# Sums of the output projection's last column block kept in PSUM between passes, and the first normalised chunks split in two halves from an fp32 copy

## The chip, the cores and the metric

The kernel runs on one core of one Trainium2 chip. The metric is the device time in microseconds of one execution, the median of several runs.

## What is computed

A two-layer encoder over 256 positions with a width of 2048, all in fp32. One layer, cut to what matters here:

```
h   = rmsnorm(x, pre_mix_norm)
proj = h @ w_in
o_a = mla_mixer(...)            # attention, 1024 channels
o_b = conformer_conv(...)       # convolution + layernorm + silu, 512 channels
o_c = gdn_mixer(...)            # gated delta rule, 512 channels
mix = concat(o_a, o_b, o_c) @ w_out
x   = x + rmsnorm(mix, post_mix_norm)
h   = rmsnorm(x, pre_ffn_norm)
f   = (silu(h @ w_gate) * (h @ w_up)) @ w_down
x   = x + rmsnorm(f, post_ffn_norm)
```

## The kernel before

Everything lies in one program. The 256 rows are two tiles of 128 (`t` = 0 and 1). Every fp32 matrix product is made of three passes on TensorE: both operands are split into a high and a low half, `hi` (a cast on ScalarE, the ACT engine, `hilo` L328) and `lo` (a subtraction on VectorE, the DVE engine, L329), and a chunk of 128 input channels takes the matmuls L353 (hi by hi), L354 (lo by hi) and L355 (hi by lo).

- `dense()` (L337) is the product of 256 rows with a block of 512 columns. A unit is two chunks: one DMA brings the weights (`ws`), ACT makes `wh` (L328, 128x1024), DVE makes `wl` (L329, 128x1024), then 12 matmuls follow. The sums lie in two PSUM tiles of the pool `psa` (four banks, tag `acc`); at the end `evac` takes them out.
- The other four PSUM banks are the pool `psb` (tag `tp`, function `TP()` L76). All transposes and all the side work of the mixer (heads, convolution, delta rule) go through these four.
- `norm_quad(t, g, ...)` (L435) transposes four 128x128 pieces of `xs` into a `tp` bank (L439), multiplies by the gain and splits the outcome. For all quads but the first this is one DVE multiply of 128x512 (L448), one cast and one subtraction (L328, L329 on 128x512). The first quad (t = 0, g = 0) goes in four columns through `hilo_col`: per column ACT L332 (scale and cast, 128x128) and DVE L333 (scale and subtract, 128x128). This happens four times: at the start, at the beginning of the FFN of both layers, and at the beginning of layer 1.
- `out_proj` (L1186 on) multiplies the joined mixer outputs by `w_out`. It goes in two passes over the 16 input chunks, four column blocks (`nb` 0 to 3) in each: pass 0 takes chunks 0 to 7 (attention), pass 1 takes 12 to 15 (delta rule) and 8 to 11 (conformer). After pass 0 the sums are copied out to SBUF (ACT L1197, one per `t`); after pass 1 DVE adds (L1200), ACT squares for the norm (L1203), DVE multiplies by the norm's weight (L1206), and after block 3 `residual` (L490) takes the reciprocal root (L262 to L270) and updates `xs` (L496, four per `t`). The product with `w_down` has one pass only.
- `conformer()` (L922) runs as background work while `out_proj` is in its first pass: 31 multiply-adds on DVE (L949), then for each `t` four transposes into a `tp` bank (L956), mean and variance (L959, L961), the root (L241 to L249) and the normalisation (L964), which reads that `tp` bank again; then eight transposes (L973), SiLU (ACT L978, with a table load), cast and subtraction. Its results are chunks 8 to 11 of `out_proj`.
- `gdn()` ends with four transposes for each `t` (L913) that fill two `tp` banks, split by ACT L332 and DVE L333 in 128x512.
- `token_sums` (L1246) takes the first quad's fp32 values by adding hi and lo again (L1251), once in a layer.

The order of the instructions on each engine is fixed when the program is built, by a scheduler with modelled costs and the pools' free buffers. An engine does its instructions strictly in that order. A weight cast can be told to be issued behind a given instruction (`hold`): at the kernel's start that is the third of the four column casts (`FH = 2`).

Of the kernel before, what the change touches and what calls it, by code (L numbers as in the profile page):

```python
# [13 lines left out]
ALU = mybir.AluOpType  # L14
# [30 lines left out]
QORDER = (4, 0, 5, 1, 6, 2, 7, 3)  # L45
EARLY = 2
UB = 64
FH = 2
SETUP_REST = 2
TURN = 1.5  # L50

# [2 lines left out]
def kernel(  # L54
# [18 lines left out]
    def U(dt=F32):  # L73
        return upool.tile([P, 512], dt, tag="u", name="u")
# [55 lines left out]
    def vcol(l, i, c):  # L130
        if l == 0 and i == PRE_MIX:
            return col0[:, c:c + 1]
        o = voff[(l, i)] + c
        return cols[:, 0, o:o + 1]
# [200 lines left out]
        return ins  # L335

    def dense(lhs, ks, n, load, evac, ch=2, need=None, pre=None, head=0, mid=None, tail=0,  # L337
              after0=None):

        acc = [psa.tile([P, 512], F32, tag="acc", name="acc") for _ in range(NT)]
        nu = -(-len(ks) // ch)
        held = []

        def mm(t, c, u, kc, wh, wl):
            i = u * ch + c
            rh = wh[:, c * n:(c + 1) * n]
            rl = wl[:, c * n:(c + 1) * n]  # L350
            xh, xl = lhs(kc[c], t)
            o = acc[t][:, 0:n]
            pe.matmul(o, xh, rh, start=(i == 0), stop=False)  # L353
            pe.matmul(o, xl, rh, start=False, stop=False)  # L354
            pe.matmul(o, xh, rl, start=False, stop=(i == len(ks) - 1))  # L355

        def unit(u):
            kc = ks[u * ch:(u + 1) * ch]
            m = len(kc)
            ws = wpool.tile([P, 1024], F32, tag="ws", name="ws", bufs=WSB)  # L360
            wv = ws[:, 0:m * n].rearrange("p (c n) -> p c n", c=m)
            load(wv, kc[0], m)
            wh = wpool.tile([P, 1024], F32R, tag="wh", name="wh", bufs=WHB)
            wl = wpool.tile([P, 1024], F32R, tag="wl", name="wl", bufs=WHB)
            with ExitStack() as order:
                if u < head:
                    for u0, ins in hold:
                        if u >= u0:
                            order.enter_context(tc.issue_after(ins.ins))
                hilo(wh[:, 0:m * n], wl[:, 0:m * n], ws[:, 0:m * n])  # L370
            if need is not None:
                for k in kc:
                    bg.ensure(*need(k))
            return u, kc, wh, wl

        for u in range(nu):
            a = unit(u)
            if head <= u < nu - tail:
                for c in range(len(a[1])):
                    for t in range(NT):  # L380
                        mm(t, c, *a)
            else:
                for c in range(len(a[1])):
                    mm(0, c, *a)
                held.append(a)
                if u == head - 1 and mid is not None:
                    mid()
                if u == nu - 1:
                    if pre is not None:
                        pre()  # L390
                        pre = None
                    evac(0, acc[0][:, 0:n])
                if u in (head - 1, nu - 1):
                    for h in held:
                        for c in range(len(h[1])):
                            mm(1, c, *h)
                    held.clear()
            bg.step(BUDGET)
        if pre is not None:
            pre()  # L400
        if after0 is not None:
            after0()
        for t in range(1 if tail else 0, NT):
            evac(t, acc[t][:, 0:n])

# [29 lines left out]
    def norm_quad(t, g, tiles, gain, keep=None):  # L435

        ps = TP()
        for c in range(4):
            pe.transpose(ps[:, c * P:(c + 1) * P], xs[:, t, (4 * g + c) * P:(4 * g + c + 1) * P], ident)  # L439
        hi, lo = U(F32R), U(F32R)  # L440
        if g == 0 and t == 0:
            for c in range(4):
                s = slice(c * P, (c + 1) * P)
                ins = hilo_col(hi[:, s], lo[:, s], ps[:, s], vcol(*gain, c))
                first_hi.append(ins)
        else:
            f = U()
            dve.tensor_tensor(out=v3(f, 4), in0=v3(ps, 4), in1=bc(gain_cols(*gain, 4 * g, 4), 2, P), op=ALU.mult)  # L448
            hilo(hi, lo, f)
            if keep is not None:  # L450
                keep[(g, t)] = f
        tiles[(g, t)] = (hi, lo)

    def ask(tiles, gain, load=None, keep=None):
# [54 lines left out]
    for l in range(DEPTH):  # L509
# [11 lines left out]

        if l == 0:
            norm_quad(0, 0, hT, (0, PRE_MIX))
            hold.append((1, first_hi[FH]))
        K16 = list(range(16))
        rxb = []

# [657 lines left out]
        def out_proj(lhs, passes, w, wpm, rname, need, after0):  # L1185
            parts = {}  # L1186
            ssqp = [SM(4, "ssqp0"), SM(4, "ssqp1")]
            for i, ks in enumerate(passes):
                last = i == len(passes) - 1
                for nb in range(4):  # L1190
                    if i == 0:
                        parts[(nb, 0)], parts[(nb, 1)] = U(), U()

                    def ev(t, ps):
                        o = parts[(nb, t)]
                        if not last:
                            act.copy(out=o, in_=ps)  # L1197
                            return
                        if i > 0:
                            dve.tensor_tensor(out=o, in0=o, in1=ps, op=ALU.add)  # L1200
                            ps = o
                        junk = U()
                        act.activation(out=junk, in_=ps, func=AF.Square, accum_out=ssqp[t][:, nb:nb + 1])  # L1203

                        def weigh():
                            dve.tensor_tensor(out=o, in0=ps, in1=wpm[nb], op=ALU.mult)  # L1206
                        if nb == 3:
                            residual(t, parts, ssqp, rname, weigh)
                        else:
                            weigh()  # L1210
                    dense(lhs, ks[nb], 512, wload(w, nb * 512, 512), ev, need=need,
                          **(dict(tail=TAILG, after0=after0) if last and nb == 3 else {}))


        a, b = list(range(8)), [12, 13, 14, 15, 8, 9, 10, 11]
        passes = [[a[:6], a, a, a], [a[6:] + b, b, b, b]]
        h2, F = {}, {}
        out_proj(lmix, passes, w_out[l], wpm, "rm", need_mix, lambda: norm_quad(0, 0, h2, (l, PRE_FFN)))


        more2 = ask(h2, (l, PRE_FFN), keep=F)
# [19 lines left out]
        def token_sums():  # L1241
# [3 lines left out]

            for g in range(4):  # L1246
                fast = [q for q in range(2) if 2 * g + q in FAST]
                if (g, 0) not in F:
                    F[(g, 0)] = U()
                    hi, lo = h2[(g, 0)]  # L1250
                    dve.tensor_tensor(out=F[(g, 0)], in0=hi.bitcast(F32), in1=lo.bitcast(F32), op=ALU.add)  # L1251
                f0, f1 = [F.pop((g, t)).rearrange("p (q j n) -> p q j n", q=2, j=2) for t in range(NT)]
                d = U()
                dve.tensor_tensor(out=d.rearrange("p (q j n) -> p q j n", q=2, j=2), in0=f0, in1=f1,
# [211 lines left out]
```

## Time and profile before

| what | value |
|---|---|
| time, median of 3 runs | 2232.72 us (2232.12 to 2234.08) |
| time of the profiled execution | 2234.14 us |
| its span in the trace | 2232.4 us |
| granted TensorE clock, mean | 0.996 |
| TensorE busy | 2202.9 us (99%) |
| VectorE busy | 1762.1 us (79%) |
| ScalarE busy | 1183.3 us (53%) |
| DMA, bytes over the span | 407.75 MB, mean 183 GB/s |

The kernel is one long stream of matmuls with few gaps. The span is the profiled execution from its first to its last instruction; its own time lies 1.7 us above it, and 1.4 us above the median of the runs. The line numbers are those of the kernel before. In the rows, PE is TensorE, DVE VectorE, ACT ScalarE; the number in brackets is idle time of that engine just before the instruction, and what ended it. Matmul records that follow each other in a stream overlap, so their distance is read from their starts.

### The profile page before, as it was taken

The numbers are of one execution on the slowest core, as the hardware profiler recorded it, in microseconds if no ns is written. First come the engines' busy times: TensorE is split into PE (matmuls) and PEld (weight loads), VectorE is DVE, ScalarE is ACT, GpSimd is POOL, SyncE is SP. The second block draws the span as 40 slices with busy tenths as digits, with TensorE's granted clock in tenths as the row PEclk, the third lists the DMA queues.
The fourth block names the chain that finished last, engine by engine and source line by source line (L and its number), as shares of the span: only waits on it lengthen the run. The fifth ranks groups of instructions, "written<-read, shape, count | busy, mean of one in ns | idle before, by whom it ended". The sixth has DMA issues, their size and how long they took to land.

```text
span 2232.4 us, 29210 instructions
## 1 busy us (share of the span) xinstructions
PE 2202.9 (99%) x10483; PEld 1841.3 (82%) x10483; DVE 1762.1 (79%) x2873; ACT 1183.3 (53%) x1642; POOL 45.6 (2%) x93
## 2 busy tenths in 40 slices
PE   8999999999999999999999999999999999999998
PEld 7988887788888888888879888877888888888886
DVE  6777998899989897544486879979989998975444
ACT  6665545555555555444356655455555555554442
POOL 2000000000000000000000000000000000000000
PEclk9999999999999999999999999999999999999999
DMA  7554624546656656555556545245566566665553
GB/s 254 172 178 146 188 95 155 163 164 209 216 180 220 223 190 221 173 194 192 179 172 187 182 142 173 96 151 161 189 203 212 191 216 213 202 213 178 191 196 124
DMA packets 218545, 407.75 MB, mean 183 GB/s; under 512 B 17607, under 2 KB 30065, under 8 KB 218400
## 3 DMA queue, kind: packets, MB, share of 16 engines
q1 hardware_dynamic: 215360, 397.72, 54.4%
q0 software_dynamic: 3008, 8.16, 1.4%
q8 instruction: 82, 1.34, 0.2%
q14 instruction: 63, 0.52, 0.1%
q10 hardware_dynamic: 32, 0.01, 0.0%
HBM read 402.94 MB, written 2.90 MB: 182 GB/s over the span
## 4 chain that ended last, share of the span: by engine, by line
PE 93%; DVE 4%; DMA 1%; ACT 1%; issue 0%; SPq 0%; DVEq 0%; ACTq 0%; POOLq 0%
PE acc L1311 19%; PE tp L1311 19%; PE acc L354 16%; PE acc L355 16%; PE acc L353 16%; DVE wl L329 1%; PE tp L1235 1%; DMA ws<-in_w_in_dram 1%; DVE xs L496 1%; DMA cd<-u 0%; PE tp L1050 0%; PE tp L796 0%; PE tp L803 0%; ACT wh L328 0%; PE tp L1021 0%
## 5 line engine op out<-in xcount | busy, mean ns | idle before, releaser
L328 ACT CAST wh<-ws 128x1024 fp32r<-128x1024 f32 (+3 forms) x820 | 816.1, 1010 | 810.8 <-PE acc L354 421.3
L329 DVE TENSOR_TENSOR wl<-ws,wh 128x1024 fp32r<-128x1024 f32 (+3 forms) x820 | 943.7, 1172 | 344.6 <-ACT wh L328 338.1
L353 PE MATMUL acc<-wh,u 128*128 128x512 f32 (+2 forms) x1792 | 696.9, 390 | 3.6 <-ACT u L328 3.2
L354 PE MATMUL acc<-wh,u 128*128 128x512 f32 (+2 forms) x1792 | 688.1, 384 | 2.9 <-DVE u L329 1.2
L355 PE MATMUL acc<-wl,u 128*128 128x512 f32 (+2 forms) x1792 | 687.1, 384 | 3.4 <-DVE wl L329 3.4
L354 PEld LDWEIGHTS acc<-wh,u 128*128 128x128 f32 x1792 | 338.6, 189 | 68.5 <-DVE u L329 4.0
L355 PEld LDWEIGHTS acc<-wl,u 128*128 128x128 f32 x1792 | 337.9, 189 | 66.8 <-DVE wl L329 4.0
L353 PEld LDWEIGHTS acc<-wh,u 128*128 128x128 f32 x1792 | 338.2, 189 | 65.4 <-ACT u L328 4.5
L1311 PE MATMUL acc<-wh,u 128*128 128x512 f32 x1220 | 376.5, 389 | 0.0
L1311 PE MATMUL tp<-wh,u 128*128 128x512 f32 x1220 | 376.0, 389 | 0.0
L1311 PEld LDWEIGHTS acc<-wh,u 128*128 128x128 f32 x1220 | 228.7, 188 | 47.9 <-DVE u L329 0.5
L1311 PEld LDWEIGHTS tp<-wh,u 128*128 128x128 f32 x1220 | 228.9, 188 | 47.6
L1311 PE MATMUL tp<-wl,u 128*128 128x512 f32 x610 | 237.4, 389 | 0.0
L1311 PE MATMUL acc<-wl,u 128*128 128x512 f32 x610 | 237.3, 389 | 0.0
L1311 PEld LDWEIGHTS acc<-wl,u 128*128 128x128 f32 x610 | 114.5, 188 | 23.7
L1311 PEld LDWEIGHTS tp<-wl,u 128*128 128x128 f32 x610 | 114.5, 188 | 23.7
L949 DVE SCALAR_TENSOR_TENSOR u<-u,cols 128x241 f32<-128x241 f32 (+14 forms) x240 | 101.9, 474 | 0.0
L1349 ACT CAST wh<-ws 128x1024 fp32r<-128x1024 f32 x60 | 63.0, 1049 | 26.6 <-PE tp L1311 11.7
L1350 DVE TENSOR_TENSOR wl<-ws,wh 128x512 fp32r<-128x512 f32 x60 | 41.2, 687 | 22.2 <-ACT wh L1349 22.2
L328 ACT CAST u<-u 128x512 fp32r<-128x512 f32 (+2 forms) x48 | 27.8, 587 | 36.8 <-DVE u L448 32.8
L1334 ACT ACTIVATE u<-u,sm 128x512 f32<-128x512 f32 x40 | 28.8, 724 | 34.6 <-DVE u L1381 24.4
L1356 DVE TENSOR_TENSOR ws<-ws 128x512 f32<-128x512 f32 x60 | 41.5, 692 | 2.0
(303 smaller groups left out, 1545.1 us busy)
## 6 DMA issues: line engine op xcount, KB each, us to landing
ws<-in_w_gate_dram SPq DMA_DIRECT2D x176, 512.0 KB, 4.9
ws<-in_w_up_dram SPq DMA_DIRECT2D x176, 512.0 KB, 4.8
ws<-in_w_down_dram SPq DMA_DIRECT2D x176, 512.0 KB, 3.6
ws<-in_w_in_dram SPq DMA_DIRECT2D x112, 512.0 KB, 4.3
ws<-in_w_out_dram SPq DMA_DIRECT2D x64, 512.0 KB, 3.7
ws<-in_w_ukv_dram SPq DMA_DIRECT2D x16, 512.0 KB, 3.6
ws<-in_w_uq_dram SPq DMA_DIRECT2D x16, 384.0 KB, 3.4
ws<-in_w_in_dram SPq DMA_DIRECT2D x10, 444.0 KB, 4.1
```

Of the source, the lines that this page charges most:

```text
L328: act.copy(out=hi, in_=src)
L329: dve.tensor_tensor(out=lo, in0=src, in1=hi.bitcast(F32), op=ALU.subtract)
L353: pe.matmul(o, xh, rh, start=(i == 0), stop=False)
L354: pe.matmul(o, xl, rh, start=False, stop=False)
L355: pe.matmul(o, xh, rl, start=False, stop=(i == len(ks) - 1))
L496: ins = dve.scalar_tensor_tensor(out=xv, in0=parts[(c, t)], scalar=r[:, 0:1], in1=xv, op0=ALU.mult, op1=ALU.add)
L949: dve.scalar_tensor_tensor(out=o, in0=i, scalar=wc, in1=o, op0=ALU.mult, op1=ALU.add)
L1311: pe.matmul(o, a, b, start=count[i] == 1, stop=count[i] == total[i])
L1334: act.activation(out=sg[t], in_=x, func=AF.Silu, scale=rfb[0][:, t:t + 1])
L1349: act.copy(out=wh, in_=wg)
L1350: dve.tensor_tensor(out=wl[:, 0:512], in0=b11, in1=wh[:, 0:512].bitcast(F32), op=ALU.subtract)
L1356: dve.tensor_tensor(out=b21, in0=b21, in1=b22, op=ALU.subtract)
```

## The change

First part: in the second half of `out_proj`'s work, block `nb == 3` of a product with more than one pass does its sums in two `tp` tiles that are kept from pass 0 to pass 1, and the matmuls of pass 1 go on adding into them. The two copies (L1197) of that block and its two additions (L1200) fall away; L1203 and L1206 read PSUM. The two banks of `psb` are held from block 3 of pass 0 until the block is done in pass 1.

Second part: the first quad is made as the others are, by one multiply of 128x512 into an fp32 tile `f`, but cast and subtracted in two halves of 128x256. `f` is kept for `token_sums`, whose addition L1251 falls away. At the kernel's start the second half's cast is the instruction that `hold` names.

```diff
     def dense(lhs, ks, n, load, evac, ch=2, need=None, pre=None, head=0, mid=None, tail=0,
-              after0=None):
+              after0=None, acc=None, first=True, last=True):
-        acc = [psa.tile([P, 512], F32, tag="acc", name="acc") for _ in range(NT)]
+        if acc is None:
+            acc = [psa.tile([P, 512], F32, tag="acc", name="acc") for _ in range(NT)]
...
-            pe.matmul(o, xh, rh, start=(i == 0), stop=False)
+            pe.matmul(o, xh, rh, start=(first and i == 0), stop=False)
             pe.matmul(o, xl, rh, start=False, stop=False)
-            pe.matmul(o, xh, rl, start=False, stop=(i == len(ks) - 1))
+            pe.matmul(o, xh, rl, start=False, stop=(last and i == len(ks) - 1))
...
+        if not last:
+            return
         for t in range(1 if tail else 0, NT):
             evac(t, acc[t][:, 0:n])
...
         hi, lo = U(F32R), U(F32R)
+        f = U()
+        dve.tensor_tensor(out=v3(f, 4), in0=v3(ps, 4), in1=bc(gain_cols(*gain, 4 * g, 4), 2, P), op=ALU.mult)
         if g == 0 and t == 0:
-            for c in range(4):
-                s = slice(c * P, (c + 1) * P)
-                ins = hilo_col(hi[:, s], lo[:, s], ps[:, s], vcol(*gain, c))
-                first_hi.append(ins)
+            for c in range(2):
+                s = slice(c * 256, (c + 1) * 256)
+                first_hi.append(act.copy(out=hi[:, s], in_=f[:, s]))
+                dve.tensor_tensor(out=lo[:, s], in0=f[:, s], in1=hi[:, s].bitcast(F32), op=ALU.subtract)
         else:
-            f = U()
-            dve.tensor_tensor(out=v3(f, 4), in0=v3(ps, 4), in1=bc(gain_cols(*gain, 4 * g, 4), 2, P), op=ALU.mult)
             hilo(hi, lo, f)
-            if keep is not None:
-                keep[(g, t)] = f
+        if keep is not None:
+            keep[(g, t)] = f
...
-                        if i > 0:
+                        if i > 0 and nb < 3:
                             dve.tensor_tensor(out=o, in0=o, in1=ps, op=ALU.add)
...
+                    two = len(passes) > 1 and nb == 3
+                    if two and i == 0:
+                        kept = [TP(), TP()]
                     dense(lhs, ks[nb], 512, wload(w, nb * 512, 512), ev, need=need,
+                          acc=kept if two else None, first=not two or i == 0, last=not two or last,
                           **(dict(tail=TAILG, after0=after0) if last and nb == 3 else {}))
...
-                if (g, 0) not in F:
-                    F[(g, 0)] = U()
-                    hi, lo = h2[(g, 0)]
-                    dve.tensor_tensor(out=F[(g, 0)], in0=hi.bitcast(F32), in1=lo.bitcast(F32), op=ALU.add)
```

The fixed order moves with it. Three places matter. In these listings a name after the line is what is written and read, and x8 is a run of eight alike; the changed kernel's own line numbers are up to three higher (L913, L956, L973 are L916, L959, L976 there, and L353 to L355 are L354 to L356), and one lower ahead of `dense` (L329 is L328).

TensorE at the end of the conformer, layer 0, before: the delta rule's transposes (L913) and, directly behind them, those of the normalisation (L956).

```order
L913 MATMUL tp<-ident,u 128x128 x8
L956 MATMUL tp<-ident,u 128x128 x4
L353 MATMUL acc<-wh,u 128x512
L956 MATMUL tp<-ident,u 128x128 x4
L353 MATMUL acc<-wh,u 128x512
L354 MATMUL acc<-wh,u 128x512
```

The same transposes in the changed kernel, the matmuls around them (L916 is 25 matmuls ahead of L959).

```order
L354 MATMUL acc<-wh,u 128x512
L355 MATMUL acc<-wh,u 128x512
L356 MATMUL acc<-wl,u 128x512
L959 MATMUL tp<-ident,u 128x128 x8
L355 MATMUL acc<-wh,u 128x512
L356 MATMUL acc<-wl,u 128x512
```

The normalisation's transposes stood behind L913 and now stand 25 matmuls later.

TensorE some 40 matmuls on, before: the transposes ahead of SiLU (L973) and the first matmuls that need their outcome, which are the `x4` at the end.

```order
L973 MATMUL tp<-ident,u 128x128 x6
L355 MATMUL acc<-wl,u 128x512
L353 MATMUL acc<-wh,u 128x512
L354 MATMUL acc<-wh,u 128x512
L355 MATMUL acc<-wl,u 128x512
L353 MATMUL acc<-wh,u 128x512
L354 MATMUL acc<-wh,u 128x512
L355 MATMUL acc<-wl,u 128x512
L353 MATMUL acc<-wh,u 128x512 x4
```

The same place in the changed kernel.

```order
L355 MATMUL acc<-wh,u 128x512
L356 MATMUL acc<-wl,u 128x512
L976 MATMUL tp<-ident,u 128x128 x8
L354 MATMUL acc<-wh,u 128x512 x4
L355 MATMUL acc<-wh,u 128x512
L356 MATMUL acc<-wl,u 128x512
```

All eight transposes now stand together, and no matmul stands between them and the four that need their outcome; before there were seven.

VectorE between `out_proj` and the FFN, layer 0, before: from the second column split on (L333), with the work on t = 1 (L262 to L270 and L1206) between them, to the first weight splits L329 in 128x1024. Ahead of this piece stand the four updates L496 for t = 0, the addition L1200 for t = 1, the first column split and a multiply L448.

```order
L333 SCALAR_TENSOR_TENSOR u<-tp,cols,u 128x128
L264 TENSOR_SCALAR sm<-sm 128x1
L267 TENSOR_SCALAR sm<-sm 128x1 x2
L269 SCALAR_TENSOR_TENSOR sm<-sm 128x1
L1206 TENSOR_TENSOR u<-u 128x512
L333 SCALAR_TENSOR_TENSOR u<-tp,cols,u 128x128
L270 SCALAR_TENSOR_TENSOR sm<-sm 128x1
L329 TENSOR_TENSOR u<-u 128x512
L333 SCALAR_TENSOR_TENSOR u<-tp,cols,u 128x128
L269 SCALAR_TENSOR_TENSOR sm<-sm 128x1
L329 TENSOR_TENSOR wl<-ws,wh 128x1024
```

The changed kernel from the four updates for t = 0 on (L445 is the multiply, L450 the two half subtractions, L328 the weight split).

```order
L499 SCALAR_TENSOR_TENSOR xs<-u,sm,xs 128x512 x4
L328 TENSOR_TENSOR wl<-ws,wh 128x1024
L445 TENSOR_TENSOR u<-tp,cols 128x512
L328 TENSOR_TENSOR wl<-ws,wh 128x1024
L450 TENSOR_TENSOR u<-u 128x256 x2
L328 TENSOR_TENSOR wl<-ws,wh 128x1024
L261 TENSOR_SCALAR sm<-sm 128x1
L1209 TENSOR_TENSOR u<-tp,u 128x512
```

Three weight splits have moved to the front, one of them ahead of the multiply and one ahead of the half subtractions; the addition for t = 1 is gone, and the second multiply (the quad g = 1) stands behind all of these.

## Rows read from the trace of the kernel before

**Rows 1.** The page: busy shares, and the chain that ended last.

```profile
PE 2202.9 (99%) x10483; PEld 1841.3 (82%) x10483; DVE 1762.1 (79%) x2873; ACT 1183.3 (53%) x1642; POOL 45.6 (2%) x93
PE 93%; DVE 4%; DMA 1%; ACT 1%; issue 0%; SPq 0%; DVEq 0%; ACTq 0%; POOLq 0%
```

**Rows 2.** TensorE's timeline, conformer's end, layer 0 (start, us, engine, line, shapes).

```profile
349.94 0.60 PE L956 MATMUL tp<-ident,u 128*128 128x128 f32 x4
361.03 0.81 PE L973 MATMUL tp<-ident,u 128*128 128x128 f32 x6
362.83 0.40 PE L354 MATMUL acc<-wh,u 128*128 128x512 f32 x1
363.06 0.40 PE L355 MATMUL acc<-wl,u 128*128 128x512 f32 x1
364.88 1.20 PE L353 MATMUL acc<-wh,u 128*128 128x512 f32 x4 [1.42 <-ACT u L328]
366.63 0.63 PE L355 MATMUL acc<-wl,u 128*128 128x512 f32 x1
369.19 0.63 PE L353 MATMUL acc<-wh,u 128*128 128x512 f32 x1
```

**Rows 3.** VectorE's timeline, the same place.

```profile
351.76 1.29 DVE L959 BATCH_NORM_STATS2 sm<-tp 128x6 f32<-128x512 f32 x2
357.79 1.23 DVE L329 TENSOR_TENSOR wl<-ws,wh 128x1024 fp32r<-128x1024 f32 x1
358.93 0.15 DVE L249 SCALAR_TENSOR_TENSOR sm<-sm 128x1 f32<-128x1 f32 x1
359.12 0.81 DVE L964 TENSOR_SCALAR u<-tp,sm 128x512 f32<-128x512 f32 x1
```

**Rows 4.** ScalarE's timeline, the same place.

```profile
361.55 1.03 ACT L978 ACTIVATE u<-tp,cols 128x256 f32<-128x256 f32 x2
363.26 1.04 ACT L328 CAST wh<-ws 128x1024 fp32r<-128x1024 f32 x1 [0.68 <-PE acc L354]
364.21 0.61 ACT L328 CAST u<-u 128x512 fp32r<-128x512 f32 x1
```

**Rows 5.** TensorE's timeline, conformer's end, layer 1.

```profile
1472.74 1.20 PE L353 MATMUL acc<-wh,u 128*128 128x512 f32 x4 [1.42 <-ACT u L328]
1474.42 0.39 PE L355 MATMUL acc<-wl,u 128*128 128x512 f32 x1
```

**Rows 6.** Timeline of all engines, from out_proj to the FFN, layer 0.

```profile
394.43 0.69 DVE L1200 TENSOR_TENSOR u<-u,acc 128x512 f32<-128x512 f32 x1 [1.79 <-PE acc L355]
400.64 0.36 ACT L332 ACTIVATE u<-tp,cols 128x128 fp32r<-128x128 f32 x1
401.06 0.50 PE L353 MATMUL acc<-wh,u 128*128 128x512 f32 x1
401.69 0.68 DVE L448 TENSOR_TENSOR u<-tp,cols 128x512 f32<-128x512 f32 x1
406.32 0.50 PE L355 MATMUL acc<-wl,u 128*128 128x512 f32 x1 [1.69 <-DVE wl L329]
```

**Rows 7.** Windows of the same stretch: busy time of each engine, granted clock, DMA.

```profile
400.00:407.00 7.00, 4.91 (x22) 2.85 (x21) 6.96 (x20) 3.14 (x8) 0.00 (x0) 1.00 0.00 0
407.00:411.00 4.00, 4.00 (x12) 3.10 (x11) 4.00 (x8) 0.62 (x1) 0.00 (x0) 0.57 0.82 242
```

**Rows 8.** TensorE's timeline at the kernel's start.

```profile
7.33 0.80 PE L353 MATMUL acc<-wh,u 128*128 128x512 f32 x1
11.68 1.54 PE L439 MATMUL tp<-ident,xs 128*128 128x128 f32 x6 [0.79 <-DMA xs<-in_x_dram]
20.99 0.40 PE L354 MATMUL acc<-wh,u 128*128 128x512 f32 x1
```

**Rows 9.** TensorE's timeline, from w_down to layer 1.

```profile
1118.25 0.50 PE L353 MATMUL acc<-wh,u 128*128 128x512 f32 x1
1124.32 0.50 PE L354 MATMUL acc<-wh,u 128*128 128x512 f32 x1 [0.97 <-DVE u L329]
```

More of the change, by code (lines that the diff above doesn't have):

```diff
@@ L47 @@
 UB = 64
-FH = 2
 SETUP_REST = 2
@@ L523 @@
             norm_quad(0, 0, hT, (0, PRE_MIX))
-            hold.append((1, first_hi[FH]))
+            hold.append((1, first_hi[1]))
         K16 = list(range(16))
@@ L1217 @@
         h2, F = {}, {}
-        out_proj(lmix, passes, w_out[l], wpm, "rm", need_mix, lambda: norm_quad(0, 0, h2, (l, PRE_FFN)))
+        out_proj(lmix, passes, w_out[l], wpm, "rm", need_mix, lambda: norm_quad(0, 0, h2, (l, PRE_FFN), F))
         more2 = ask(h2, (l, PRE_FFN), keep=F)
```

## The prediction

> **What bounds the kernel now.** The page comes first: TensorE is busy 99% of the span and holds 93% of the chain that ended last [rows 1]. So nothing that ACT or DVE saves counts in itself; the change can only move TensorE's gaps. I therefore compared the fixed order on each engine and looked in the timelines at the places where it differs: the end of the conformer and the step from out_proj to the FFN (both layers), the step from w_down to layer 1, and the start. Everywhere else TensorE's order is the same.
>
> At full clock, matmuls start 0.23 us apart (362.83 and 363.06) [rows 2]. After some waits they start 0.43 us apart: six between 366.63 and 369.19 [rows 2]. That is the lower of the two clock levels, 1.2 instead of 2.4 GHz, and each such matmul loses 0.20 us.
>
> **Removed work.** Per layer two ACT copies and two DVE adds (L1200, 0.69 us [rows 6]) go, and the add of token_sums goes. Outside of the places below they run beside TensorE's stream, which covers them: 0 us.
>
> **Conformer's end (twice).** Two of the four tp banks are now held from block 3 of pass 0, and the delta rule's transposes fill the other two. The transposes for the layernorm (L956) therefore stand 25 matmuls later. Before, they started at 349.94 [rows 2]; 25 matmuls of 0.227 us are 5.7 us, and they start at some 355.7 and end, eight of them at about 0.11 us, at 356.6.
> The DVE chain behind them began with the statistics at 351.76 and ended with the normalisation (L964), for t = 0 at 359.12 [rows 3]. In the new order it has two statistics (1.29 together), three weight splits (1.23 in the row, 1.14 from start to start), some 25 small steps of 0.10 (two lie between 358.93 and 359.12), and two L964 of 0.77, all from [rows 3]: 1.2 + 3.4 + 2.5 + 1.5 = 8.7 us, from 356.65 to 365.3. The third weight split now stands between the two L964.
> TensorE's transposes (L973) need both. Before, the last of them started at 361.03 as a group of six and seven matmuls came behind it, as cover (1.6 us); then TensorE waited 1.42 us until the casts for the first conformer chunk were there, at 364.88 [rows 2]. Now all eight stand together with no matmul behind, so TensorE reaches them at about 362.1, waits, and ends them at 366.1. Then come the two SiLU of the first pair (1.03 together) and a cast (0.61) [rows 4], so the matmul that stood at 364.88 starts at 367.55. The weight cast of 1.04 at 363.26, which held that cast up before [rows 4], no longer stands between; this is in the sum. **Loss: 2.7 us per layer, 5.4 in all.** Ends: 1.3 if half of the lateness is made up by DVE finding its weight splits ready sooner, 4.3 if the cover lost (1.6) comes on top.
> The clock: after its 1.42 us wait layer 0 ran about ten matmuls at the lower level (to 369.19 and a little on [rows 2]), 2.0 us; layer 1 had the same wait and was back at 0.23 by 1474.42 [rows 5], 0.2 us. The new wait is longer (some 4.6 us in three pieces). I take the same two losses, so 0; ends −2.0 and +1.8 (layer 1 falls as layer 0 did).
>
> **From out_proj to the FFN (twice).** The addition at 394.43 goes, 0.69 us at the head of the chain to xs [rows 6], and xs for t = 0 is ready 0.7 us sooner. Before, the first matmul could start when one column was split: ACT L332 at 400.64, 0.36 us, matmul at 401.06 [rows 6]. Now a weight split of 1.2 may stand in the way, then the multiply (0.68, as L448 [rows 6]) and a cast of 128x256, taken between the 0.36 of a 128x128 and the 0.61 of a 128x512 [rows 4, 6], some 0.42: the first matmul starts at 402.4, 1.3 later. In return the four columns no longer hand back and forth between ACT and DVE, and the weight splits stand ahead of the work on t = 1, so the wait of 1.69 us for wl at 406.32 [rows 6] goes. TensorE then waits for the second quad instead: 12 matmuls to 405.95, the quad's halves at 407.2 and 408.5. By the start of the t = 1 matmuls (417.8 before) it is 0.85 us ahead, if the clock stays up. Before, it did not: the window from 407 to 411 has a granted clock of 0.57 [rows 7], about eight matmuls or 1.7 us. Those new waits are shorter each but not less in sum, so I take half of that: 0.85 − 0.85 = **0 us**; ends −0.85 and +0.85 per layer.
> The Trainium skill, page "Perfetto Trace Analysis", section "Optimizing Scalar/DVE Operations", says that where ScalarE and VectorE are not saturated but cause bubbles elsewhere, breaking instructions up may let work finish sooner. By it, halving the pieces from four to two would cost what the later first matmul shows, about 1.3 us in each layer; I don't follow it because the row at 406.32 shows the weight split and not the column pieces as the last wait.
>
> **From w_down to layer 1 (once).** The matmul at 1118.25 moves to about 1119.5 for the same reason, without a saved add. The waits here were small (0.97 at 1124.32 [rows 9]), and most of the delay is made up in them: **0.4 us**; ends 0 and 1.3.
>
> **Start (once).** Eleven transposes now stand ahead of the first matmul, and the last three wait for the transfer that landed at 11.68 [rows 8]. The matmuls that ran from 7.33 on move behind it. Six of them at the lower clock are 2.6 us, the upper end. But then nothing is missing: 27 matmuls (6.2 us), 20 transposes (2.5) and about 1.1 for the lower clock from 11.68 on give 21.5, against 20.9 [rows 8]: **0.6 us**; lower end −0.3.
>
> **Sum.** 5.4 + 0 + 0.4 + 0.6 = 6.4 us over the profiled execution's own time of 2234.14 us. That execution is 1.42 above the median of 2232.72; on the median: 2239.1 us. A difference of 0.2%, 4.5 us, is about what a measurement can tell from none.
>
> **Rivals.**
> *The conformer's delay is hidden* and the sum stays below 4.5. For it: the lower clock in layer 0 might not come back (−2.0), and DVE's chain had pieces in which it waited for weight casts. With the lower ends, 2 × 1.3 + 0.4 + 0.6 = 3.6, or 1.9 with the handover's gain: 2234.6 to 2236.3. Against it: TensorE's order has no matmul left to put in the gap.
> *Faster.* The one mechanism is the handover: if the new order takes away its waits and the clock stays up, each layer gets back the idle 2.1 us of the window from 400 to 407 [rows 7] and the 1.7 us behind it, 7.6 in two layers. With the conformer's loss at 0 and the start and layer 1 at 1.0 this is −6.6: 2226.1. It decides only if the transposes L973 are not later than before, which needs DVE to have normalised both tiles by 360.8; the statistics alone start 4.9 us later. Little speaks for it.
> *Banks in the way all along.* The Trainium skill, page "Perfetto Trace Analysis", section "Matmul Optimizations", asks that all eight PSUM banks be used for parallel work, which speaks against holding two of them. As a mechanism of this kernel: two tp banks also have to serve the last heads between block 3 of pass 0 and its end in pass 1, some 45 us per layer; if each conformer step loses the cover (4.3) and the clock falls in both layers (1.8) and at both handovers (1.7), it is 8.6 + 1.8 + 1.7 + 1.0 = 13.1: 2245.8.
>
> **Numbers.** The forecast, with a sum between 4.5 and 10, has 0.52; the hidden delay and what else lies within 0.2% has 0.32; faster 0.08; the larger loss 0.08. Slower is then 0.60. The range leaves out most of the faster case and the top of the largest: 2231.5 to 2245.
>
> **What would show it.** In the changed profile: statistics L959 some 5 us later against the same matmul, L973's transposes waiting for DVE L964 in two pieces of 1 to 2 us, and then a wait for ACT of about 1.4; at the handover no wait of 1.7 for wl, but waits of about 1 for the second quad. If the gap ahead of SiLU's matmuls is under 2 us in all, the main term is wrong; if matmuls elsewhere between 370 and 394 wait for a tp bank, the banks count for more than I took.

## The result: 2245.16 us against 2233.4, and the profile after

The changed kernel takes 2245.16 us (median of 4 runs, 2244.04 to 2246.25); the kernel before, run beside it, 2233.4 (2232.12 to 2235.91). The ratio is 1.0053, 95% interval 1.004 to 1.0065: slower by 11.8 us. The direction was forecast; the size was not. 6.4 us were forecast, and the time lies 0.2 us above the upper end of the range.

The page of the changed kernel answers to [rows 1]:

```profile
PE 2204.8 (98%) x10483; PEld 1845.4 (82%) x10483; DVE 1760.5 (78%) x2863; ACT 1178.2 (52%) x1630; POOL 46.0 (2%) x93
PE 95%; DVE 3%; DMA 1%; ACT 1%; issue 0%; SPq 0%; DVEq 0%; ACTq 0%; POOLq 0%
```

TensorE does the same 10483 matmuls. DVE and ACT are less busy, by 1.6 and 5.1 us, and the span is 12.1 us longer: the work removed was covered, and TensorE's gaps grew.

To see where, I took TensorE's instructions by number (the 1000th of one trace against the 1000th of the other), and the lateness of each over the kernel before, as a median over quiet stretches, in which it stays the same. How much it grows from one quiet stretch to the next is what the place between them costs. All runs below are told in this way; the totals are those of one profiled execution each. The start is read at about 300 us, and there it holds one thing more: the first profile of before has a wait of 0.48 us at 138 us that most others lack, so that they gain 0.6 to 0.7 us there. Read at 100 us, the changed kernel is 3.4 us late.

| us, against the first profile of before | start | conformer 0 | to FFN 0 | w_down to layer 1 | conformer 1 | to FFN 1 | all |
|---|---|---|---|---|---|---|---|
| forecast | 0.6 | 2.7 | 0 | 0.4 | 2.7 | 0 | 6.4 |
| changed kernel | 2.6 | 4.3 | −0.6 | 0.6 | 4.3 | 0.9 | 12.1 |

The conformer, layer 0, TensorE in the changed kernel; this answers to [rows 2]. The last two groups are the transposes ahead of SiLU and the first users of its outcome.

```profile
359.00 1.04 PE L959 MATMUL tp<-ident,u 128*128 128x128 f32 x8
...
364.87 0.39 PE L356 MATMUL acc<-wl,u 128*128 128x512 f32 x1
366.79 0.30 PE L976 MATMUL tp<-ident,u 128*128 128x128 f32 x1 [1.54 <-DVE sm L248]
368.63 0.98 PE L976 MATMUL tp<-ident,u 128*128 128x128 f32 x7 [1.53 <-DVE u L967]
370.93 2.08 PE L354 MATMUL acc<-wh,u 128*128 128x512 f32 x4 [1.32 <-ACT u L327]
372.80 0.63 PE L355 MATMUL acc<-wh,u 128*128 128x512 f32 x1
373.23 0.63 PE L356 MATMUL acc<-wl,u 128*128 128x512 f32 x1
```

The three waits are the ones that were forecast, 4.4 us together against 1.4 (and 0.3) before. In layer 1 the first of them is shorter, and they come to 4.0:

```profile
1478.60 0.30 PE L976 MATMUL tp<-ident,u 128*128 128x128 f32 x1 [1.14 <-DVE sm L248]
1480.43 0.98 PE L976 MATMUL tp<-ident,u 128*128 128x128 f32 x7 [1.53 <-DVE u L967]
1482.74 1.62 PE L354 MATMUL acc<-wh,u 128*128 128x512 f32 x3 [1.32 <-ACT u L327]
```

With every wait over 0.05 us counted, TensorE's idle time at the conformer grows from 2.0 to 4.7 us in layer 0 and from 2.0 to 4.3 in layer 1. VectorE in layer 0, answering to [rows 3]: the third weight split stands between the two normalisations, as worked out.

```profile
365.84 0.81 DVE L967 TENSOR_SCALAR u<-tp,sm 128x512 f32<-128x512 f32 x1
366.56 0.15 DVE L248 SCALAR_TENSOR_TENSOR sm<-sm 128x1 f32<-128x1 f32 x1
366.63 1.22 DVE L328 TENSOR_TENSOR wl<-ws,wh 128x1024 fp32r<-128x1024 f32 x1
367.76 0.81 DVE L967 TENSOR_SCALAR u<-tp,sm 128x512 f32<-128x512 f32 x1
```

What was not forecast follows the waits. These are windows of the changed kernel (the columns are those of [rows 7]; the number behind POOL's is the granted clock):

```profile
370.00:377.00 7.00, 6.07 (x15) 4.83 (x16) 1.39 (x2) 2.51 (x6) 0.00 (x0) 0.51 0.10 38
377.00:380.00 3.00, 3.00 (x15) 2.44 (x14) 1.95 (x3) 1.20 (x2) 0.00 (x0) 1.00 0.00 0
411.00:414.50 3.50, 3.50 (x10) 2.63 (x8) 3.50 (x11) 0.62 (x1) 0.00 (x0) 0.51 0.85 234
1127.50:1131.50 4.00, 3.98 (x11) 2.62 (x9) 4.00 (x12) 0.62 (x1) 0.00 (x0) 0.57 0.82 226
1482.50:1486.50 4.00, 3.76 (x10) 2.98 (x11) 1.38 (x2) 1.72 (x4) 0.00 (x0) 0.57 0.03 9
1527.00:1530.50 3.50, 3.50 (x15) 2.88 (x13) 3.50 (x6) 0.18 (x1) 0.00 (x0) 0.52 0.39 137
```

A granted clock of 0.5 is the lower level, 1.2 GHz. In the kernel before, the records have three low stretches ahead of the last one at the kernel's end, each 3.4 us long: behind the first conformer, and at both steps to the FFN. The changed kernel has five, one of them (from 370.05 to 376.88) twice as long. Eight matmuls at 0.43 instead of 0.23 us are 1.6 us, so one 3.4 us stretch costs about 1.6, less where TensorE would have waited during it anyway; the three more come to 4.8 of the 12.1 us at most. This is an estimate from the spacings.

The start, TensorE in the changed kernel, answers to [rows 8]:

```profile
12.58 0.90 PE L442 MATMUL tp<-ident,xs 128*128 128x128 f32 x3 [5.17 <-DMA xs<-in_x_dram]
13.14 0.78 PE L354 MATMUL acc<-wh,u 128*128 128x512 f32 x1
...
17.98 0.63 PE L354 MATMUL acc<-wh,u 128*128 128x512 f32 x1
18.41 0.43 PE L355 MATMUL acc<-wh,u 128*128 128x512 f32 x1
18.68 0.40 PE L356 MATMUL acc<-wl,u 128*128 128x512 f32 x1
```

The wait for the transfer is 5.17 us, nothing fills it, and behind it the matmuls stay 0.43 us apart until 18.4.

The step to the FFN of layer 0, TensorE (see [rows 6]): the wait of 1.69 for wl is gone, and waits for the cast and the subtraction of the half quads are there instead.

```profile
409.21 0.50 PE L354 MATMUL acc<-wh,u 128*128 128x512 f32 x1 [1.23 <-ACT u L449]
410.24 0.50 PE L355 MATMUL acc<-wh,u 128*128 128x512 f32 x1 [0.53 <-DVE u L450]
```

### The profile page after: what moved, and what is told of

It is laid out like the page before. It is cut to its first block, busy times and chain, and to the rows that moved or that the text cites. A ratio compares the mean times of both kernels' runs of the same rounds, so it can differ in the third digit from the quotient of the medians.

```text
span 2244.5 us, 29198 instructions
## 1 busy us (share of the span) xinstructions
PE 2204.8 (98%) x10483; PEld 1845.4 (82%) x10483; DVE 1760.5 (78%) x2863; ACT 1178.2 (52%) x1630; POOL 46.0 (2%) x93
## 4 chain that ended last, share of the span: by engine, by line
PE 95%; DVE 3%; DMA 1%; ACT 1%; issue 0%; SPq 0%; DVEq 0%; ACTq 0%; POOLq 0%
PE acc L1314 18%; PE tp L1314 18%; PE acc L354 16%; PE acc L355 16%; PE acc L356 16%; DVE wl L328 1%; PE tp L1242 1%; PE tp L442 1%; PE tp L354 1%; PE tp L356 1%; PE tp L355 1%; PE tp L1053 1%; PE tp L806 0%; PE tp L799 0%; PE tp L1024 0%; DMA xs<-in_x_dram 0%
## 5 line engine op out<-in xcount | busy, mean ns | idle before, releaser
L328 DVE TENSOR_TENSOR wl<-ws,wh 128x1024 fp32r<-128x1024 f32 (+3 forms) x820 | 943.8, 1172 | 349.3 <-ACT wh L327 342.1
L354 PE MATMUL acc<-wh,u 128*128 128x512 f32 (+2 forms) x1728 | 673.5, 391 | 7.6 <-ACT u L449 3.7
L355 PE MATMUL acc<-wh,u 128*128 128x512 f32 (+2 forms) x1728 | 664.5, 385 | 3.2 <-DVE u L328 1.7
L356 PE MATMUL acc<-wl,u 128*128 128x512 f32 (+2 forms) x1728 | 663.7, 384 | 0.0
L354 PEld LDWEIGHTS acc<-wh,u 128*128 128x128 f32 x1728 | 327.5, 190 | 67.2 <-ACT u L327 4.7
L355 PEld LDWEIGHTS acc<-wh,u 128*128 128x128 f32 x1728 | 327.2, 189 | 64.4 <-DVE u L328 4.5
L356 PEld LDWEIGHTS acc<-wl,u 128*128 128x128 f32 x1728 | 326.6, 189 | 60.9
L1314 PEld LDWEIGHTS acc<-wh,u 128*128 128x128 f32 x1220 | 228.7, 188 | 47.7 <-DVE u L328 0.5
L1314 PEld LDWEIGHTS acc<-wl,u 128*128 128x128 f32 x610 | 114.5, 188 | 23.9
```

What stands on the lines that cost most here:

```text
L328: dve.tensor_tensor(out=lo, in0=src, in1=hi.bitcast(F32), op=ALU.subtract)
L354: pe.matmul(o, xh, rh, start=(first and i == 0), stop=False)
L356: pe.matmul(o, xh, rl, start=False, stop=(last and i == len(ks) - 1))
L1314: pe.matmul(o, a, b, start=count[i] == 1, stop=count[i] == total[i])
```

## The experiments

The theory after this look: two held tp banks make the loss at the conformer, the first quad's new form makes the loss at the start and from w_down to layer 1, and each longer wait can bring stretches at the lower clock that cost as much again. The rivals are named with each run. All of them, in the columns of the table above; "low" counts the stretches of 3.4 us at the lower clock between the start and the end (one of 6.8 counts as two).

| run | start | conf. 0 | FFN 0 | w_down | conf. 1 | FFN 1 | all | low | median us (before beside it) |
|---|---|---|---|---|---|---|---|---|---|
| changed kernel | 2.6 | 4.3 | −0.6 | 0.6 | 4.3 | 0.9 | 12.1 | 6 | 2245.16 (2233.4) |
| e1 sums only | −0.1 | 3.0 | −1.2 | 0 | 5.7 | −1.3 | 6.6 | 4 | 2239.95 (2233.14) |
| e2 first quad only | 1.7 | −1.6 | 0.2 | 2.3 | 0.3 | 0.0 | 3.3 | 3 | 2237.02 (2233.14) |
| e3 one bank | 1.2 | 1.2 | −0.3 | 2.3 | 1.4 | −0.5 | 5.9 | 2 | 2239.91 (2233.14) |
| e4 start in columns | 0.1 | 3.6 | −0.5 | 0.7 | 5.8 | −0.3 | 9.3 | 7 | 2242.55 (2233.14) |
| e5 banks held only | −1.1 | 2.0 | 0 | 0 | 3.3 | 0 | 4.1 | 3 | 2238.98 (2232.68) |
| e6 one bank, columns | −0.6 | −0.3 | −0.7 | 0 | 1.3 | −0.9 | −1.2 | 0 | 2236.18 (2232.68) |
| e7 changed again | 1.6 | 3.7 | −0.6 | 0.7 | 5.4 | −0.6 | 10.7 | 7 | 2244.78 (2232.68) |
| e8 before again | −0.7 | 0 | 0 | 0 | 0 | 0 | −0.1 | 3 | 2234.02 (2232.68) |
| e9 woven | −0.9 | 1.8 | 0 | 0 | 3.3 | 0.2 | 4.3 | 5 | 2236.78 (2232.8) |

(Small drifts of up to 0.6 us between the places are in the sum alone.)

**e1: the first part alone.** The edit is shown against the changed kernel; the addition of `token_sums` is back too, and the cast named by `hold` is the third column's again.

```diff
-        f = U()
-        dve.tensor_tensor(out=v3(f, 4), in0=v3(ps, 4), in1=bc(gain_cols(*gain, 4 * g, 4), 2, P), op=ALU.mult)
         if g == 0 and t == 0:
-            for c in range(2):
+            for c in range(4):
...
+                ins = hilo_col(hi[:, s], lo[:, s], ps[:, s], vcol(*gain, c))
```

> First part alone: the two kept banks, with the first quad still split in four columns and the addition of token_sums left in. Theory (the loss at the conformer comes from the two held tp banks, the loss at the start from the first quad): against the kernel before, the same matmul is 0.0 to 0.3 us later at 100 us, 4.3 us later after the conformer of layer 0 and again of layer 1, and the handover to the FFN gives back 0 to 0.7 per layer; in all +7 to +9 us. Rival (the first quad's new form moves the order at the conformer too): under +3 us, with the layernorm's transposes directly behind those of the delta rule.

Measured: ratio 1.0028 (1.0019 to 1.0038), 6.8 us, a little under the 7 to 9 expected. Nothing at the start; 3.0 and 5.7 at the conformers, the same three waits as in the changed kernel, and −1.2 at each step to the FFN. The rival falls: the transposes stand 25 matmuls later here too. Both conformers are followed by a low stretch of 6.8 us; neither step to the FFN has one, which is where the −1.2 come from: the kernel before has one of 1.6 there.

**e2: the second part alone.** The edit against the kernel before; `hold` and `token_sums` are as in the changed kernel.

```diff
-            for c in range(4):
-                s = slice(c * P, (c + 1) * P)
-                ins = hilo_col(hi[:, s], lo[:, s], ps[:, s], vcol(*gain, c))
-                first_hi.append(ins)
+            for c in range(2):
+                s = slice(c * 256, (c + 1) * 256)
+                first_hi.append(act.copy(out=hi[:, s], in_=f[:, s]))
+                dve.tensor_tensor(out=lo[:, s], in0=f[:, s], in1=hi[:, s].bitcast(F32), op=ALU.subtract)
```

> Second part alone: the first quad as one multiply and two halves, sums copied and added as before. Theory: +2.7 us at the start (six matmuls moved behind the third transfer of xs, and the lower clock for longer), 0 at the conformers, +0.6 from w_down to layer 1, and between -0.5 and +1 at each handover to the FFN; in all +2.5 to +5 us. Rival (the start's loss of 2.7 was the transfer, which landed 0.9 us later in that execution by chance): +1.5 or less at 100 us.

Measured: ratio 1.0016 (1.0007 to 1.0026), 3.9 us. The start costs 1.7, and 2.5 read at 100 us, where the expectation was 2.7 and the rival at most 1.5. The step from w_down to layer 1 costs 2.3, more than the 0.6 expected:

```profile
1119.88 0.50 PE L352 MATMUL acc<-wh,u 128*128 128x512 f32 x1 [1.23 <-ACT u L445]
1120.91 0.50 PE L353 MATMUL acc<-wh,u 128*128 128x512 f32 x1 [0.53 <-DVE u L446]
...
1124.67 0.49 PE L352 MATMUL acc<-wh,u 128*128 128x512 f32 x1 [0.97 <-ACT u L327]
1125.95 0.50 PE L353 MATMUL acc<-wh,u 128*128 128x512 f32 x1 [0.79 <-DVE u L328]
...
1127.53 0.63 PE L352 MATMUL acc<-wh,u 128*128 128x512 f32 x1
```

Where the kernel before had one wait of 1.0 there [rows 9] and smaller ones, 1.9 us together, four stand in a row, 3.5 us together, and then a low stretch. The low stretch alone does not make the 2.3: the changed kernel has one there as well, and TensorE's order between the two is the same. But there the lower clock begins right behind the first two waits, at 1127.81, and the last two, 0.97 and 0.79 here, shrink to one:

```profile
1131.92 0.50 PE L355 MATMUL acc<-wh,u 128*128 128x512 f32 x1 [0.44 <-DVE u L328]
```

So it matters where the lower clock begins: behind the second wait it takes time in which TensorE would have waited (0.6 in all), behind the fourth it comes on top (2.3). At the first conformer the time falls by 1.6 with the order and the idle time as before: only its low stretch is missing. The steps to the FFN show nothing gained by the second part; TensorE's idle time there grows from 2.0 to 2.7 us.

**e3: one bank instead of two.** The edit against the changed kernel:

```diff
-                        kept = [TP(), TP()]
+                        kept = [TP(), None]
...
-                        if i > 0 and nb < 3:
+                        if i > 0 and not (nb == 3 and t == 0):
```

(`None` takes an accumulator from `psa`, and the flags `first` and `last` are given for each t.)

> The changed kernel, but only the sums of t = 0 are kept in a tp bank; those of t = 1 are copied out and added as before, so one bank is held instead of two. Theory (number of free tp banks): three free banks let the first tile's transposes for the layernorm stand where they stood before, and six matmuls or more stand between the last transposes ahead of SiLU and their users; the conformer costs 0 to 2 us per layer instead of 4.3, and the whole is 4 to 9 us under the changed kernel. Rival (the loss comes from the accumulation over two passes or from a busier VectorE): still over 3.5 us at each conformer.

Measured: ratio 1.0028 (1.0017 to 1.0038); 1.2 and 1.4 at the conformers, 5.2 us under the changed kernel in the median. One tile's transposes stand where they stood, the other's 25 matmuls later, as the theory has it. The cover that it expected is not there: no matmul stands between the last transposes ahead of SiLU and their users, and TensorE waits twice.

```profile
365.31 0.87 PE L975 MATMUL tp<-ident,u 128*128 128x128 f32 x6 [1.40 <-DVE u L966]
367.80 2.07 PE L354 MATMUL acc<-wh,u 128*128 128x512 f32 x4 [1.62 <-ACT u L327]
```

The idle time grows by 1.1 us at each conformer, against 2.2 to 2.7 in the changed kernel. The rival's 3.5 is not seen; but since this kernel also keeps the sums of one tile only, it does not tell the bank from the sums. e5 does.

**e4: the changed kernel with the start as before.** The edit against the changed kernel:

```diff
+        if g == 0 and t == 0 and gain == (0, PRE_MIX):
+            for c in range(4):
+                s = slice(c * P, (c + 1) * P)
+                first_hi.append(hilo_col(hi[:, s], lo[:, s], ps[:, s], vcol(*gain, c)))
+            tiles[(g, t)] = (hi, lo)
+            return
...
-            hold.append((1, first_hi[1]))
+            hold.append((1, first_hi[2]))
```

> The changed kernel, but the first quad at the kernel's start (only there) is split in four columns as before. Theory: the 2.7 us at the start go and nothing else moves: the changed kernel less 2.4 to 3.0 us. Rival (late transfer): less 0 to 1 us.

Measured: 2.6 us less in the median, and 0.1 instead of 2.6 at the start. The start's loss hangs on the first quad's form. Its size varies: read at 100 us, the four executions with halves lost 3.4, 2.5 (e2), 1.9 (e3) and 2.2 (e7), those with columns stand between −0.4 and 0.2. The means are 2.5 and 0.0, so it costs about 2.5 us, and some 0.9 of the 3.4 of the first profile was chance: the transfer landed at 12.58 there, and at 11.69, 11.86 and 12.22 in the others.

**e5: the banks held, and nothing else.** The edit against the kernel before:

```diff
+                    if two and i == 0:
+                        kept = [TP(), TP()]
+                        for k in kept:
+                            dve.memset(k[:, 0:1], 0.0)
...
+                    if two and last:
+                        for k in kept:
+                            dve.tensor_tensor(out=SM(1, "held"), in0=k[:, 0:1], in1=ssqp[1][:, 3:4], op=ALU.add)
```

> The kernel before, with two tp banks taken at block 3 of pass 0 and given back after block 3 of pass 1; nothing is summed in them (one column is cleared, and read at the end), and sums are copied and added as before. Theory (the held banks alone make the loss at the conformer): the layernorm's transposes stand 25 matmuls later as in the changed kernel, waits at each conformer come to about 4.5 us instead of 2.1, and with stretches at the lower clock each conformer costs 3 to 6 us; the handover to the FFN is as before or up to 0.5 later; in all +6 to +11 us. Rival (the accumulation over two passes or the missing copies do it): under +2 us in all.

Measured: ratio 1.0028 (1.0018 to 1.0038), 6.3 us, with no sum kept. TensorE's transposes there:

```profile
355.45 1.04 PE L956 MATMUL tp<-ident,u 128*128 128x128 f32 x8
362.81 0.30 PE L973 MATMUL tp<-ident,u 128*128 128x128 f32 x1 [0.84 <-DVE sm L248]
363.82 0.98 PE L973 MATMUL tp<-ident,u 128*128 128x128 f32 x7 [0.71 <-DVE u L964]
```

They stand as late as in the changed kernel (24 matmuls behind L913) and wait in the same two pieces. So the banks alone move the transposes and make the three waits. They do not make the whole loss: the waits ahead of SiLU are 0.84 and 0.71 where the changed kernel has 1.1 to 1.5 and 1.53, the idle time grows by 1.4 us at each conformer instead of 2.2 to 2.7, and the conformers cost 2.0 and 3.3 instead of 4.3 each. The first is under the 3 to 6 expected. VectorE shows the difference in the second wait:

```profile
361.85 0.81 DVE L964 TENSOR_SCALAR u<-tp,sm 128x512 f32<-128x512 f32 x1
...
362.96 0.81 DVE L964 TENSOR_SCALAR u<-tp,sm 128x512 f32<-128x512 f32 x1
363.68 1.22 DVE L329 TENSOR_TENSOR wl<-ws,wh 128x1024 fp32r<-128x1024 f32 x1
```

The two normalisations start 1.11 us apart here, with the weight split behind them, and 1.92 apart in the changed kernel (and 1.93 in e1), where the weight split stands between them. That 0.8 us comes with the kept sums, through the order that the scheduler chose, and not with the banks.

**e6: one bank and columns.** The edit is e3's on the kernel of e1 (the flags go as in e3):

```diff
-                        kept = [TP(), TP()]
+                        kept = [TP(), None]
```

> First part alone with one bank: only the sums of t = 0 are kept, the first quad goes in four columns as before. If the parts add up: 0 at the start and at w_down, +1.2 us at each conformer (as in e3), -1.2 at each handover (as in e1): within 1.5 us of the kernel before. If the conformer's loss with one bank hung on the first quad's form: another number than +1.2 there, by over 1 us.

Measured: the profiled execution is 1.2 us under the kernel before, and its records have no low stretch at all until the end. The median of its ten runs is 2236.18 (2232.93 to 2237.6), ratio 1.0015 (1.0005 to 1.0025): the profiled execution is the fastest of its kernel and not a typical one. The expected 1.5 us of the kernel before hold for it and not for the median, which is 3.5 us above. Against the first conformer's 1.2 expected stands −0.3, since the kernel before has its low stretch there (1.6) and this one none; at the second, where neither has one, it is 1.3, as expected. The steps to the FFN give back 0.7 and 0.9 of the 1.2. So the idle times add up (1.1 us more at each conformer, as in e3); the time of an execution does not: the records put the low stretches at other places.

**e7 and e8: the two kernels once more.**

> The changed kernel once more, for its profile. Theory (waits are fixed by the order, the number of stretches at the lower clock behind them varies from execution to execution): the idle time at each place is the same within 0.3 us, and the lower clock's share differs by one or two stretches of about 1.6 us somewhere. Rival (every execution has the same stretches): both the same within 0.3 us.

> The kernel before once more, for its profile. Theory: the same idle times at each place within 0.3 us; the stretches at the lower clock behind the conformers and the handovers (one, one, none, one in the first profile) differ in one place or more. Rival: the same stretches at the same places.

Measured for e7: the waits at the second conformer agree with the first profile; at the first they are 0.4 us shorter, the last of the three being 0.91 instead of 1.32. Low stretches are seven instead of six, one long one behind each conformer, and the second conformer costs 5.4 instead of 4.3. The step to the second FFN gives −0.6 instead of 0.9, with one low stretch in either profile and TensorE's order the same. There the idle time differs, 2.2 against 3.5 us, more than the 0.3 expected. In e7 the lower clock begins at 1521.66, right behind the wait of 0.53 at 1520.99, and one wait of 0.44 follows; in the first profile it begins at 1527.17, behind two waits more:

```profile
1524.63 0.50 PE L354 MATMUL acc<-wh,u 128*128 128x512 f32 x1 [0.95 <-ACT u L327]
1525.91 0.50 PE L355 MATMUL acc<-wh,u 128*128 128x512 f32 x1 [0.78 <-DVE u L328]
```

This is the difference of e2 over again. So the stretches move between executions, and the waits behind them change with it. For e8 the theory was wrong: the same three stretches at the same places, and the time of each place within 0.1 us, but for the wait at 138 us, which this execution lacks (0.7). With two profiles of each, the changed kernel's stretches are seen to vary, those of the kernel before are not.

**e9: more cover at the conformer.** Pass 1 of the kernel before, with its first two blocks woven:

```diff
+                    n0 = len(ks[0]) - 4
+                    steps[:2] = [(0, ks[0][:n0], True, False), (1, ks[1][:4], True, False),
+                                 (0, ks[0][n0:], False, True), (1, ks[1][4:], False, True)]
...
```

> No bank held and the first quad in columns, as in the kernel before; instead the start of pass 1 is woven: block 0 does chunks 6, 7 and 12 to 15, then block 1 its chunks 12 to 15, and only then both take the conformer's chunks 8 to 11. If 24 matmuls of block 1 then stand between the transposes ahead of SiLU and the first user of the conformer's output, the wait of 1.4 us there goes (idle at each conformer under 1 us instead of 2.1) and with it the lower clock behind it: 3 to 6 us under the kernel before in all. Rival (the scheduler sets the conformer's transposes as late as their user, so the cover does not grow): the same idle time as before and within 1.5 us of the kernel before.

Measured: a miss, ratio 1.0015 (1.0006 to 1.0025), 4.0 us above the kernel before. The scheduler set the eight transposes directly ahead of their user, as the rival has it, but the rival's time, within 1.5 us of the kernel before, was missed too:

```profile
360.94 1.04 PE L977 MATMUL tp<-ident,u 128*128 128x128 f32 x8
364.99 2.07 PE L355 MATMUL acc<-wh,u 128*128 128x512 f32 x4 [3.01 <-ACT u L328]
```

It shows something else. No bank is held here and the transposes do not wait, but no matmul stands behind them: the wait is 3.01 instead of 1.42 [rows 2]. The 1.6 us more agree with the seven matmuls of 0.23 that stood there before. Together with the wait of 0.3 ahead of the transposes, which is gone here, the idle time grows by 1.1 us at each conformer. So of the 2.2 to 2.7 us of idle time that the changed kernel has more there, 1.1 may go with that cover, and the rest with the later normalisation. That the two add up in this way is argued and not shown.

None of the versions run is faster than the kernel before.

## Why the prediction was half right

**Right.** The mechanism and its place: the held banks move the layernorm's transposes 25 matmuls back, SiLU's transposes lose the matmuls behind them, a weight split comes between the normalisations, and the three waits come to 4.4 us (4.0 in layer 1, 3.9 and 4.0 in e7) where 4.6 was said. The net of the waits was put at 2.7 us per layer; the idle time grew by 2.7 and 2.2 us, in e7 by 2.2 and 2.3. That the removed copies and adds are worth 0 agrees with the page: DVE and ACT are 1.6 and 5.1 us less busy, and the span is longer. No run takes that work away by itself. The step from w_down was put at 0.4 and came to 0.6 and 0.7 in the changed kernel's two profiles; e2 and e3, with the same order there, lost 2.3. At the steps to the FFN the wait for wl went and waits for the halves came.

**Wrong: the clock behind the conformer, taken as 0.** I took the losses of the kernel before as they stood (2.0 in layer 0, 0.2 in layer 1), although the new wait was three times as long, and put the upper end at 1.8 for layer 1 alone. Measured, the conformers come to 4.3 and 4.3, in the second profile to 3.7 and 5.4. Of these 8.6 and 9.1 us, 4.9 and 4.5 are idle time, less than the 5.4 of the sum. The rest, 3.7 and 4.6, stands where the sum has 0, and goes with low stretches: one more in each layer, in the second profile two more in layer 1, which at 1.6 each are 3.2 and 4.8. The rival "Banks in the way all along" (2245.8, with a chance of 0.08) came nearest to the time, and by luck: its 4.3 per conformer was waits and lost cover, with 1.8 for the clock on top, and its shortage for the last heads is not seen: up to 345 us the lateness stays at 2.6, and from 378 to 398 us TensorE has no wait at all.

**Wrong: the start, sized at 0.6.** I moved the matmuls behind the transfer and gave the lower clock 1.1 us from there on. In the changed kernel the spacing of 0.43 lasts to 18.4: ten matmuls and seven transposes, which by their spacings are some 2.7 us. With the transfer 0.9 us later, 0.6 + 1.6 + 0.9 = 3.1, which is the lateness at 30 us. Over all runs the start costs 2.5, near the upper end of 2.6. With halves the loss follows the time at which the records show the full clock: 18.5, 17.5, 16.4 and 16.2 us go with losses of 3.4, 2.5, 2.2 and 1.9 at 100 us. With columns it does not: the full clock comes at 14.9 in before, 10.8 in e8 and 16.6 in e6, and they lie within 0.3 us of each other.

**Right by its mean, not by its reasons: the steps to the FFN, 0.** In the changed kernel they give −0.6 and 0.9, and −0.6 twice in e7, with a low stretch at each in both profiles: half of the clock was taken as regained, none was. The first part alone (e1) does regain it, −1.2 each; that the first quad's halves, with their waits of 1.23 and 0.53, spend it again is argued: e3 has the wait of 1.23 too, and no low stretch at either step.

The two mis-sized terms make the difference: 3.2 and 3.7 at the conformers, and 2.0 and 1.0 at the start as the table reads it, over a sum of 6.4.

**The two rules weighed.** With the sums kept, the halves cost over the columns what lies between e1's −1.2 at each step to the FFN and the changed kernel's −0.6 and 0.9: 0.6 and 2.2 us (0.6 and 0.7 in e7). Without kept sums they cost nothing there (e2: 0.2 and 0.0). As far as the stretches at the lower clock move by themselves, part of either pair is chance. The Trainium skill's page "Perfetto Trace Analysis", section "Optimizing Scalar/DVE Operations", that breaking instructions up may let work finish sooner, agrees with the numbers with kept sums and not with those of e2 at these steps; I was wrong to set it aside for the changed kernel as a whole. Holding banks costs 2.0 and 3.3 us at the conformers with no other edit (e5). With the section "Matmul Optimizations" of the same page of the Trainium skill, that all eight banks are to be used, this agrees.

## What to carry to other kernels

A PSUM bank that is kept to save an addition is paid for by whoever next needs a bank: look in TensorE's order for transposes that come later, and count the matmuls left between them and their users. Where TensorE is busy 99% of the time, price each new wait twice: once by its length, and once by the matmuls at the lower clock that may follow, which vary from one execution to the next, and in what they cost with the place where the lower clock begins. A smaller count of instructions on engines off the critical path says nothing about the time.

## What was not expected of the hardware

The lower clock came in stretches of about 3.4 us or twice that: in before from 366.5 to 369.9, in the changed kernel from 370.05 to 376.88, in e1 from 364.8 to 371.6. Waits of the same length brought it or not: the kernel before has 2.0 us of idle time at both conformers, and a low stretch behind the first alone, in both of its profiles. In e6, with 3.1 us at each, there is none. Which of two alike waits brings it was not settled; no run here could set the clock.
